# The order of the last steps before the output projection: scores of attention heads 2 and 3 ahead of the projection of the values

## The chip, the cores and the metric

The kernel runs on one core of one Trainium2 chip. The metric is the device time of one execution in microseconds (us), compared by the median of several runs. The engines are PE (TensorE: matmuls, PEld for its weight loads), DVE (VectorE), ACT (ScalarE), POOL (GpSimd) and SP (SyncE, which here issues nearly all DMAs).

## The reference

One layer of a sequence encoder on 512 tokens of 2048 features. The input is scaled and shifted by vectors computed from a condition `c` (a matrix product with `ada_w`), projected by `w_in`, and the projection is cut into the inputs of four mixers of 512 features each. Their outputs are concatenated, projected by `w_out`, gated, added to the input and normalised; a feed-forward block follows.

```python
h = x * (1.0 + scale1) + shift1
proj = h @ w_in[l]
...
o_a = _hgrn2(...)            # cat[0:4]   four heads of 128
o_b = _s5(...)               # cat[4:8]
o_c = _stick_breaking(sb_q, sb_k, sb_v)   # cat[8:12]  four heads of 128
o_d = _rwkv7(...)            # cat[12:16]
mix = jnp.concatenate([o_a, o_b, o_c, o_d], axis=-1) @ w_out[l]
x = _layer_norm(DEEPNORM_ALPHA * x + gate1 * mix, ln1_g[l], ln1_b[l])
```

The mixer that the change touches is the third, in blocks of 128 queries:

```python
z = einsum('bhtd,bhsd->bhts', q, k)          # q already times 128 ** -0.5
log_rest = where(mask, log_sigmoid(-z), 0)   # mask: key before query
after = cumsum(log_rest, reverse=True) - log_rest
w = where(mask, exp(log_sigmoid(z) + after), 0)
o = einsum('bhts,bhsd->bhtd', w, v)
```

## The kernel before, in words

All matrices are float32. A projection is made of three matmuls for each pair of tiles: both operands are split into a rounded part and a rest (`hi` by an ACT cast, `lo` by a DVE subtraction), and `mm3` (L592) multiplies hi by hi, lo by hi and hi by lo. `wload` (L580) loads a 256 KB piece of weights by one DMA from SP into one of three buffers `wr`, then splits it into `wh` and `wl`, three buffers each.

The kernel is written as a list of steps, the string `ORDER` (L40, L41), and the loop at L1456 issues them in that order; a number behind a colon is `E.rate`. The program's instructions are then ordered by a planner: an instruction has the place at which it was issued as its priority, `high_priority(offset=n)` moves it n places ahead, and on each engine the planner takes, by its own estimate of times, the first in priority of those that are ready and have a buffer. An engine then works through its own list strictly in that order. Weight loads and splits stand 500 places ahead (`E.ahead`), the four heads of the first mixer 1500 (`BEFORE`, "H").

The steps around the change:

- `K<h>`: `qk(h)` (L1396), queries and keys of attention head h. Two calls of `proj_fm` (L1172), each 48 matmuls into one PSUM bank `pd` with 4 weight loads; the banks are emptied by ACT into `qT` and `kT` in the pool `pp` (16 buffers).
- `VS`: `proj_tm` (L1184) for the values of all four heads: 192 matmuls with 16 weight loads, four `pd` banks (all there are) held from the first to the last, emptied by four ACT copies into `tm` (pool `pp`). In the trace its matmuls read `pd<-wh,hh` and the like, those of `K<h>` `pd<-hh,wh`.
- `A<p>`: `sb_scores` (L1007) for heads 2p and 2p+1. Matmuls of 16 records in five banks `pm` give the scores, which ACT copies into five tiles `sz`; DVE adds the mask, ACT takes Abs, Exp and Ln into five tiles `sl`, DVE makes max and sum, sums them up by scans and subtracts, ACT takes the last Exp. The two small tiles `one` make all Ln wait for the last Exp before them, and the last Exp for the scans. The tiles `sz` and `sl` are ten of the 34 buffers of the pool `tp`; `sz` is kept for `B<p>`.
- `B<p>`: `sb_values` (L1049): 20 transposes of `sz`, copied by ACT to `swT`, and matmuls of 40 records with the values; the result is `cat[8+2p]` and the next.
- `H<h>`: a head of the first mixer. Seven levels, each a DVE subtraction `hd`, two ACT Exp into `hx`, two DVE products, 4 matmuls (in eight records) and a masked DVE copy into `hP`. `L<p>` takes their logarithms (ACT Ln) ahead of that. `TAIL` (`hg_tail`, L993) normalises the four outputs.
- The condition's product with `ada_w` is a queue `E.bg` of 224 entries: 192 steps of one DMA `aw` and one DVE operation `acc` each, 12 ends, and 20 empty ones. `pump` (L1154) hands out `E.rate` entries behind every weight load of a projection; `PUMP` empties the queue. An end takes a `pd` bank for a moment.
- `W1`, `W2`: `w_out` (L1420). For each of four column blocks, four `pd` banks take eight (W1) or four (W2) tiles of `cat`; DVE multiplies each bank by the gate into `go` and adds it to `acc`, which frees the bank.

By the rates in `ORDER`, 168 of the 224 entries are handed out up to and including `K0`.

Of the kernel before, what the change touches and what calls it, by code (L numbers as in the profile page):

```python
# [37 lines left out]
START = "M0 E0 G0 C0 g2 M1 S0 g6 F0 M2 S1 g1 E1"  # L38

ORDER = ("k3 xg:3 r1:1 v1 k2:1 v3 r3:3 v0:2 S5 r2 r0:1 KEYS SUB INV v2:3 V:1 R12:3 R4:3 CHAIN F2:1 F1:2 F3:1 "  # L40
         "R0:2 F0 K1:2 L0 H0 H1 K0:2 L1 H2 H3 VS:2 A0 K3:2 K2:2 PUMP TAIL B0 A1 W1:2 B1 W2")  # L41

BEFORE = {"S5": 600, "KEYS": 600, "SUB": 300, "INV": 1000, "CHAIN": 1500, "H": 1500}

# [1811 lines left out]
```

## Time and profile before

| | us |
|---|---|
| median of 3 runs | 2546.42 (2540.97 to 2553.87) |
| profiled execution, its own time | 2543.48 |
| its span, first to last instruction | 2541.5 |
| PE busy | 2437.8 |
| DVE busy | 1730.7 |
| ACT busy | 955.5 |
| mean granted TensorE clock | 0.980 |

Matmuls overlap, so busy PE time is more than the time the matrix unit needs for them; a matmul of 512 columns lasts 0.39 us and the next starts 0.23 us after it. "Idle before, releaser" behind a row is time in which the engine did nothing before it, and what ended that.

In the span, `K1` and `K0` end with the copies of their keys at 724.6 and 766.5 us, the four heads `H0` to `H3` run from about 712 to 833 us, `VS` from 755 to 833 us, `A0` begins at 835 us, `K3` and `K2` run from 833 to 885 us, the score matmuls of `A1` stand at 896 to 901 us, and `W1` has its first matmul at 890.9 us.

### The profile page before, as it was taken

To read this page: it belongs to the slowest core of one execution; us is meant where nothing else is said; L and a number is where in the kernel's file an instruction comes from. 1 tells how busy PE (TensorE), PEld (TensorE's weight loads), DVE (VectorE), ACT (ScalarE), POOL (GpSimd) and SP (SyncE) were. 2 spreads that over 40 slices of the span, in tenths; PEclk is the share of its full clock that TensorE was granted. 3 is DMA by queue.
4 is the path that set the end of the run, shared out by engine and by line. 5 is a ranking of instruction groups with operands and counts; after the bars stand their busy time and mean duration, and the time that the engine had idled before them with its cause. 6 is when DMAs were issued, how large, how long until landed. Compare 5 with 4: busy or idle time off the path is not lost. (4 is left out here: it accounts for less than half of the span.)

```text
span 2541.5 us, 33306 instructions
## 1 busy us (share of the span) xinstructions
PE 2437.8 (96%) x11890; PEld 1897.7 (75%) x11890; DVE 1730.7 (68%) x2673; ACT 955.5 (38%) x1406; POOL 131.4 (5%) x293
## 2 busy tenths in 40 slices
PE   8999999999999999989999999999999999999996
PEld 3557767776788778867777877787778788788885
DVE  3755987357689975788787778777877744536227
ACT  2435242322454654164444444434443421121122
POOL 3300000010000000000000000000000000000000
PEclk9999999899999999999999999999999999999998
DMA  9876324334744554336666566655665788869632
GB/s 294 258 245 199 92 75 126 103 116 145 227 130 137 167 173 133 125 100 208 219 208 206 180 203 214 201 182 197 208 204 192 258 321 294 300 206 315 225 117 82
DMA packets 328877, 481.83 MB, mean 190 GB/s; under 512 B 44962, under 2 KB 151676, under 8 KB 328712
## 3 DMA queue, kind: packets, MB, share of 16 engines
q1 hardware_dynamic: 317976, 452.78, 55.3%
q0 software_dynamic: 8480, 26.27, 2.7%
q8 instruction: 93, 1.52, 0.3%
q10 hardware_dynamic: 2256, 0.67, 0.1%
q14 instruction: 72, 0.59, 0.1%
HBM read 445.51 MB, written 34.10 MB: 189 GB/s over the span
## 5 line engine op out<-in xcount | busy, mean ns | idle before, releaser
L102 ACT CAST wh<-wx 128x1024 fp32r<-128x1024 f32 (+1 forms) x416 | 401.2, 970 | 735.9 <-PE p L93 348.7
L105 DVE TENSOR_TENSOR wl<-wx,wh 128x1024 fp32r<-128x1024 f32 (+1 forms) x416 | 457.5, 1119 | 264.4 <-ACT wh L102 262.1
L102 ACT CAST wh<-wr 128x512 fp32r<-128x512 f32 x236 | 145.5, 618 | 329.2 <-PE pd L93 224.7
L123 DVE SCALAR_TENSOR_TENSOR acc<-aw,cact,acc 128x512 f32<-128x512 f32 x240 | 179.8, 749 | 123.6 <-DMA aw<-in_ada_w_dram 120.3
L93 PE MATMUL pt<-wl,gh 128*128 128x512 f32 x640 | 249.3, 390 | 2.1 <-DVE wl L105 1.8
L93 PE MATMUL pt<-wh,gh 128*128 128x512 f32 x640 | 249.1, 389 | 0.0
L93 PE MATMUL pt<-wh,gl 128*128 128x512 f32 x640 | 249.0, 389 | 0.0
L105 DVE TENSOR_TENSOR wx<-wx 128x512 f32<-128x512 f32 (+1 forms) x264 | 225.1, 866 | 28.6 <-DMA wx<-in_ffn_w_dram 26.9
L105 DVE TENSOR_TENSOR wl<-wr,wh 128x512 fp32r<-128x512 f32 x236 | 162.0, 689 | 113.3 <-ACT wh L102 96.2
L93 PE MATMUL pd<-hh,wl 128*128 128x512 f32 x512 | 205.6, 402 | 5.6 <-DVE wl L105 5.5
L93 PE MATMUL pd<-hh,wh 128*128 128x512 f32 x512 | 207.6, 407 | 2.4 <-ACT hh L102 2.4
L93 PE MATMUL pd<-hl,wh 128*128 128x512 f32 x512 | 204.0, 399 | 0.0
L93 PE MATMUL p<-wl,hdh 128*128 128x512 f32 x352 | 140.6, 404 | 20.0 <-DVE wl L105 20.0
L93 PE MATMUL p<-wh,hch 128*128 128x512 f32 x336 | 137.1, 408 | 16.4 <-DVE g L105 12.3
L93 PE MATMUL p<-wh,hdh 128*128 128x512 f32 x352 | 141.8, 403 | 1.1 <-ACT u L102 1.1
L93 PEld LDWEIGHTS pt<-wl,gh 128*128 128x128 f32 x640 | 120.1, 188 | 28.6 <-DVE wl L105 4.0
L93 PE MATMUL p<-wh,hdl 128*128 128x512 f32 x352 | 141.3, 402 | 0.0
L93 PEld LDWEIGHTS pt<-wh,gh 128*128 128x128 f32 x640 | 120.2, 188 | 25.6 <-ACT wh L102 0.8
L93 PEld LDWEIGHTS pt<-wh,gl 128*128 128x128 f32 x640 | 120.2, 188 | 25.1
L93 PE MATMUL p<-wl,hch 128*128 128x512 f32 x336 | 135.7, 404 | 0.3 <-DVE wl L105 0.3
L93 PE MATMUL p<-wh,hcl 128*128 128x512 f32 x336 | 135.0, 402 | 0.0
L93 PE MATMUL p<-wl,hbh 128*128 128x512 f32 x336 | 132.2, 393 | 0.8 <-DVE wl L105 0.8
(530 smaller groups left out, 4535.3 us busy)
## 6 DMA issues: line engine op xcount, KB each, us to landing
wx<-in_ffn_w_dram SPq DMA_DIRECT2D x592, 256.0 KB, 3.4
aw<-in_ada_w_dram SPq DMA_DIRECT2D x384, 256.0 KB, 4.6
wr<-in_w_in_dram SPq DMA_DIRECT2D x184, 256.0 KB, 3.3
wx<-in_ffn_w_dram SPq DMA_DIRECT2D x44, 1024.0 KB, 6.1
gh<-gd SPq DMA_DIRECT2D x88, 256.0 KB, 5.3
gl<-gd SPq DMA_DIRECT2D x88, 256.0 KB, 6.2
wr<-in_w_out_dram SPq DMA_DIRECT2D x64, 256.0 KB, 3.0
gd<-gh POOLq DMA_DIRECT2D x44, 256.0 KB, 4.1
```

Source lines behind the costliest of these rows:

```text
L93: return self.nc.tensor.matmul(out=out, lhsT=lhsT, rhs=rhs, start=start, stop=stop, **kw)
L102: self.nc.scalar.copy(out=out, in_=in_)
L105: self.nc.vector.tensor_tensor(out=out, in0=a, in1=b, op=op)
L123: self.nc.vector.scalar_tensor_tensor(out=out, in0=a, scalar=s, in1=b, op0=op0, op1=op1)
```

## The change

`VS` is taken from behind `H3` and put behind `TAIL`; `A1` is taken from behind `B0` and put behind `K2`. Nothing else is changed: every step, its rate and its code stay.

```diff
 ORDER = ("k3 xg:3 r1:1 v1 k2:1 v3 r3:3 v0:2 S5 r2 r0:1 KEYS SUB INV v2:3 V:1 R12:3 R4:3 CHAIN F2:1 F1:2 F3:1 "
-         "R0:2 F0 K1:2 L0 H0 H1 K0:2 L1 H2 H3 VS:2 A0 K3:2 K2:2 PUMP TAIL B0 A1 W1:2 B1 W2")
+         "R0:2 F0 K1:2 L0 H0 H1 K0:2 L1 H2 H3 A0 K3:2 K2:2 A1 PUMP TAIL VS:2 B0 W1:2 B1 W2")
```

So the steps behind `H3` read: before `VS A0 K3 K2 PUMP TAIL B0 A1 W1`, after `A0 K3 K2 A1 PUMP TAIL VS B0 W1`.

## Prediction

> **What bounds the kernel now.** I read the page first, for the engine whose list fills the span.
>
> ```profile
> span 2541.5 us, 33306 instructions
> PE 2437.8 (96%) x11890; PEld 1897.7 (75%) x11890; DVE 1730.7 (68%) x2673; ACT 955.5 (38%) x1406; POOL 131.4 (5%) x293
> ```
>
> PE is the bound, so the change is worth the idle PE time that it takes away or adds, no more. The second view is therefore who made PE wait; of its rows these lie near the moved steps.
>
> ```profile
> PE pd L93 <- ACT sz L99: 5.1, 1, 5.1
> PE pm L96 <- DVE ho L105: 2.0, 2, 1.3
> ```
>
> The columns are total, times and longest. The first is one wait, the longest single one in that view, and it stands beside `A1`. The timeline of PE there, and that of DVE in the same microseconds:
>
> ```profile
> 921.98 0.39 PE L93 MATMUL pd<-wl,cath 128*128 128x512 f32 x1
> 927.51 0.76 PE L93 MATMUL pd<-wh,cath 128*128 128x512 f32 x1 [5.14 <-ACT sz L99]
> 928.08 0.63 PE L93 MATMUL pd<-wh,catl 128*128 128x512 f32 x1
> ...
> 931.92 0.50 PE L93 MATMUL pd<-wh,catl 128*128 128x512 f32 x1
> 932.26 0.39 PE L93 MATMUL pd<-wl,cath 128*128 128x512 f32 x1
> 932.48 0.39 PE L93 MATMUL pd<-wh,cath 128*128 128x512 f32 x1
> ```
>
> ```profile
> 919.55 2.96 DVE L126 TENSOR_TENSOR_SCAN sl<-ones,sl 128x256 f32<-128x256 f32 x4
> 922.43 0.13 DVE L118 TENSOR_SCALAR one<-sl 128x1 f32<-128x1 f32 x1
> 922.47 0.69 DVE L105 TENSOR_TENSOR sz<-sz,sl 128x512 f32<-128x512 f32 x1
> ...
> 923.67 2.50 DVE L105 TENSOR_TENSOR sz<-sz,sl 128x512 f32<-128x512 f32 x4
> 926.08 0.69 DVE L105 TENSOR_TENSOR wl<-wr,wh 128x512 fp32r<-128x512 f32 x1
> 926.68 1.29 DVE L105 TENSOR_TENSOR go<-pd,g 128x512 f32<-128x512 f32 x2
> ```
>
> The releaser named on PE's row is the exponential of `A1`, but no matmul of `W1` reads it. What PE needs at 927.51 is an empty bank: the first column block of `W1` has filled all four `pd`, and the operation that empties them, `go`, stands on DVE behind the scans and subtractions of `A1`, which come earlier in `ORDER` and so have the better priority. `go` starts at 926.68, its first half ends near 927.4, and PE goes on. After the pause matmuls follow each other by 0.43 us until 931.92 (928.08, 928.50 and so on), and by 0.23 us from 932.26.
>
> The other wait, a little earlier:
>
> ```profile
> 885.17 1.14 PE L93 MATMUL pm<-rs,selC 32*128 32x512 f32 x8
> 887.63 1.25 PE L96 MATMUL pm<-ident,sz 128*128 128x128 f32 x8 [1.32 <-DVE ho L105]
> 889.61 1.53 PE L96 MATMUL pm<-ident,sz 128*128 128x128 f32 x12 [0.73 <-DVE ho L105]
> ```
>
> `TAIL` fills the `pm` banks with its broadcasts (`rs,selC`), DVE empties them by the products `ho`, and the transposes of `B0` wait for them. The projections are over at 885, so PE has little else.
>
> **The change part by part.**
>
> *`A1` ahead of `W1` by the length of `VS`.* `A1` needs `K2`, and before it had only `B0` and the first block of `W1` beside it.
>
> ```profile
> 896.49 4.48 PE L93 MATMUL pm<-kT,qT 128*128 128x512 f32 x16
> ```
>
> From these score matmuls to the resumed matmul at 927.51 the chain takes 31 us. Afterwards `K2` should end near 838 (`K3` and `K2` take the place of `VS`, which ended at 833, and `A0`'s scores add 4.5), and `A1` near 869. `VS` follows it with 192 matmuls, 44 us at 0.23, then `B0` and the first block of `W1`, and only then the first `go`, with DVE free of `A1`. Gained: the idle 5.14 us, and the slow restart: 11 starts from 927.51 to 932.26 took 4.75 us, where 0.23 us apiece make 2.50, so 2.25 us.
>
> *`VS` behind `TAIL`.* The broadcasts of `TAIL` and the products `ho` now have `VS` on PE beside them, so the transposes of `B0` find their banks free: gained 1.32 + 0.73 = 2.05 us. If `TAIL` came too late for that cover, these 2.05 would stay.
>
> *What fills PE under the heads.* Until 833 `VS` was the filler between the levels of `H1` to `H3`; now `K3` and `K2` are.
>
> ```profile
> core 0: us, PE busy (x) PEld busy (x) DVE busy (x) ACT busy (x) POOL busy (x), PEclk, DMA share, GB/s
> 767.00:835.00 68.00, 68.00 (x386) 56.51 (x384) 60.40 (x116) 31.64 (x68) 0.53 (x1) 1.00 0.46 134
> 835.00:890.00 55.00, 52.69 (x241) 41.12 (x241) 50.46 (x93) 35.77 (x61) 0.00 (x0) 1.00 0.58 176
> 890.00:928.00 38.00, 32.75 (x164) 26.28 (x163) 33.65 (x62) 29.58 (x50) 0.00 (x0) 0.96 0.59 190
> ```
>
> Both fillers have 192 matmuls, 16 DMAs of 256 KB on SP, 16 casts on ACT and 16 subtractions on DVE, at the same spacing: nothing on PE, and on SP's queue 16 loads exchanged for 16. The queue of `ada_w`: 168 entries are gone before, and the next 32 (with 32 DMAs `aw` on SP and 32 `acc` on DVE) go beside `K3` and `K2` instead of `VS`, again under the heads; `PUMP` finds 24 entries, of which two are steps and two ends, so hardly anything comes out in one heap. POOL's queue has no part in it. Cost: zero, hidden by the same fillers; if that cover failed, a late load would cost PE what it is late.
>
> *`A0` under `H2` and `H3`.* This is the new load. Its inputs are there at 766.5:
>
> ```profile
> L102 ACT COPY kT<-pd x1: 581/581/581, 766.5 to 766.5; 128x512 f32<-128x512 f32 x1
> 835.00:871.00 36.00, 12.60 (x20) 9.05 (x15) 1.00 0.62 190
> L105 DVE TENSOR_TENSOR sz<-sz,negm x16: 284/288/294, 837.1 to 905.2; 128x128 f32<-128x128 f32 x16
> L102 ACT COPY sz<-pm x10: 586/586/592, 836.5 to 901.0; 128x512 f32<-128x512 f32 x10
> L99 ACT ACTIVATE sz<-sz,one x10: 707/718/725, 867.0 to 926.8; 128x512 f32<-128x512 f32 x10
> ```
>
> The second row is the stretch in which `A0` ran, for the instructions on the tiles `sl` alone (DVE 12.60, ACT 9.05); the other rows are for `A0` and `A1` together, in ns, so half of each is added: 8 x 0.288 = 2.3 for DVE and 5 x 0.586 + 5 x 0.718 = 6.5 for ACT. That is 15 us of DVE and 16 of ACT. From 767 to 835 DVE has 68 - 60.40 = 7.6 us free, ACT 36. So the heads and `A0` together end some 8 us later than the heads did alone. PE does not pay for that as such: what it lacks in head matmuls it takes from the 384 filler matmuls of `K3`, `K2`, `VS`. The heads' result is needed by `W2` only, behind the 384 matmuls of `W1` (88 us at 0.23).
>
> But ACT's functions get mixed. What a change of function costs:
>
> ```profile
> 846.24 0.63 ACT L99 ACTIVATE sl<-sl 128x512 f32<-128x512 f32 x1
> 846.89 1.28 ACT L99 ACT_TABLE_LOAD   x1
> 848.19 0.72 ACT L99 ACTIVATE sl<-sl,one 128x512 f32<-128x512 f32 x1
> ...
> 862.84 1.28 ACT L99 ACT_TABLE_LOAD   x1
> ```
>
> A load ahead of the first Ln, another ahead of the next Exp. Before 846.89 the last load is at 706.88: no Ln stood among the Exps of the heads. There, where two loads stood just ahead of a head (`H0`), PE waited for its first level:
>
> ```profile
> 703.61 1.28 ACT L99 ACT_TABLE_LOAD   x1
> 706.88 1.28 ACT L99 ACT_TABLE_LOAD   x1
> 714.14 1.10 PE L93 MATMUL pm<-hx 128*128 128x64 f32 x8 [1.98 <-DVE hx L105]
> ```
>
> PE's list is fixed, eight filler matmuls (1.9 us) between two levels, so it can't go on with a filler when a level is late. Bounds: no cost, if the five Ln of `A0` fall behind the last head or between two heads; at most five pairs of loads, 10 x 1.28 = 12.8 us, if each Ln has a head's Exp on both sides and PE pays every load. Below nothing there is no room, since PE was busy all 68 us of that window. I take one pair at the nearest row's price, 1.98 us, since the five Ln become ready together and ACT is less than half busy. The Trainium skill, "ScalarE: Activation LUTs", section "What ACT_TABLE_LOAD costs", gives 2.66 us for a switch with its drain; by that the upper bound would be 26.6 us, an estimate from that page. The rows above do not agree: the operation before the load was over by then (846.24 + 0.63), and the next starts 1.30 us behind the load's start. The same page, "Table sets: the hidden batching unit", knows a set with both exp and ln, by which the cost would be zero; the two loads around the Ln of `A0` show that this program does not use it.
>
> *Handovers.* `VS` now hands its four `pd` banks to `W1`. Its ACT copies `tm` are of the form of `sz<-pm` (0.586), and the last matmuls of the four banks are 0.7 us apart; the 20 transposes of `B0` (1.25 + 1.53 us in the rows above) lie between. Cost zero, if ACT is free of `A1` then. The buffers of `tp`: `A1`'s five `sl` are free 40 us before the 16 `acc` of `W1` want them, before they were not.
>
> **The sum**, against the profiled execution's own 2543.48: -5.14 - 2.25 - 2.05 + 1.98 = -7.46, which makes 2536.0. The median of the runs lies 2.94 above that execution, so the forecast of the median is 2539.0.
>
> **The rivals.**
>
> *The wait moves.* If `A0` and the heads crowd each other so much that `A1` starts 15 us late, it ends near the end of `VS`, and ACT's copies `tm` or DVE's first `go` stand behind it as they do now. Then only the 2.05 us go: 2544.4. For it: DVE lacks 8 us in the window. Against: 8 is half of 15, and `K2` needs only PE and the splits, which stand 500 places ahead.
>
> *The heads' Exps are cut by Ln: slower.* Place: levels of `H2` and `H3` from 768 on. Price 1.28 us a load on PE; with ten, -9.44 + 12.8 = +3.4, 2549.8. It decides against the change from eight loads on (9.44 / 1.28 = 7.4). For it: ACT is idle 36 us of 68 between the pairs of `hx`, so Ln fits there one by one, and PE's list has no slack. Against: the planner may place Ln in one group. By the skill's price of a switch, named above, this rival would end at 2563.6, an estimate.
>
> *Nothing is moved in effect.* The planner works by readiness, so if `A0` finds no ten buffers in `tp` beside the heads, its chain starts at 835 as before, `A1` follows later, and the gain is the 2.05 of `TAIL` or less: 2544.4 to 2546.4. For it: a head has some ten tiles in `tp`, the finished outputs and gates another dozen. Against: `A1` would still have `VS` behind it.
>
> **How the numbers follow.** Forecast 0.5, the wait moves 0.15, Ln among Exp 0.2, nothing in effect 0.15. 0.5% is 12.7 us, about what a measurement of this kernel can tell from no change; -7.46 and all rivals lie within it. Faster than that needs the full 9.44 and another 3 us, which the spread of the runs (5.45 below the median) or a further wait that falls away could give: 0.16. Slower by that needs the far end of the Ln rival and more: 0.08. Range: low by the full gain and that spread, 2546.42 - 9.44 - 5.45 = 2531.5; high by the Ln rival, 2549.8, and a little beyond, 2551.
>
> **What would show it.** Right: no PE wait over 1 us between 835 and 950; `go` of `W1` directly behind the last matmul of its bank; score matmuls of `A1` followed by `pd<-wh,hh`; `TAIL`'s products beside `VS`. Wrong: more than four table loads between 767 and 880 with PE waits for `hx` in `H2` and `H3`; a wait for `tm` or `go` at the first matmuls of `W1`; `A0` still at 835. The far parts (feed-forward) should keep their length; if they don't, the planner has changed more than these steps, and the sum says nothing of that.

## The result and the profile after

| | median, us | profiled execution | its span |
|---|---|---|---|
| before, 4 runs | 2546.26 (2540.97 to 2553.87) | 2543.48 | 2541.5 |
| after, 4 runs | 2581.81 (2574.28 to 2586.52) | 2582.68 | 2580.7 |

The ratio is 1.0137, with a 95% interval of 1.0115 to 1.0158. The change made the kernel slower by 35.6 us; the forecast was a gain of 7.5. The page of the kernel after, its span and PE's row:

```profile
span 2580.7 us, 33297 instructions
PE 2444.7 (95%) x11890; PEld 1901.5 (74%) x11890; DVE 1733.1 (67%) x2673; ACT 956.0 (37%) x1406; POOL 131.4 (5%) x293
```

PE has the same 11890 instructions and DVE the same 2673, so the 39.2 us of span are not more work. Who made PE wait (total, times, longest) now begins with a row that the kernel before does not have:

```profile
PE pd L93 <- DVE acc L123: 30.8, 1, 30.8
```

That is one wait of 30.8 us. PE's timeline around it:

```profile
832.80 1.04 PE L93 MATMUL pm<-hsq,ones 128*32 128x512 f32 x2
833.78 2.42 PE L93 MATMUL pm<-kT,qT 128*128 128x512 f32 x7
...
844.13 0.95 PE L93 MATMUL pd<-ones,acc 128*128 128x1 f32 x8
846.28 3.72 PE L93 MATMUL pm<-kT,qT 128*128 128x512 f32 x12 [1.20 <-ACT kT L102]
851.23 1.13 PE L93 MATMUL pm<-kT,qT 128*128 128x256 f32 x4 [1.24 <-ACT sz L102]
883.16 1.87 PE L93 MATMUL pd<-ones,acc 128*128 128x1 f32 x8 [30.79 <-DVE acc L123]
884.89 0.77 PE L93 MATMUL pd<-wh,hh 128*128 128x512 f32 x1
```

`hsq,ones` at 832.80 is the end of `H3`, and `A0`'s scores follow it; they did not go under the heads. `K2` is over at 844, `A1`'s scores at 852. Then PE does nothing until `pd<-ones,acc`, an end of the `ada_w` queue, and right behind the end stand the first matmuls of `VS` (`pd<-wh,hh`). `VS` is the only large work left for PE there, and its first weights were long ready: the first three splits `wl` of `VS` ended at 840.3, 843.9 and 847.0 (with three buffers there can be no more). What it lacked, by this reading, was a bank: `VS` holds all four `pd`, and the end, which the `PUMP` ahead of it had issued, was to have one of them first. The experiments below test that. DVE shows why the end came so late:

```profile
851.97 5.83 DVE L126 TENSOR_TENSOR_SCAN sl<-ones,sl 128x512 f32<-128x512 f32 x8
...
869.89 0.75 DVE L123 SCALAR_TENSOR_TENSOR acc<-aw,cact,acc 128x512 f32<-128x512 f32 x1
870.55 3.09 DVE L123 SCALAR_TENSOR_TENSOR sl<-sz,sl 128x512 f32<-128x512 f32 x5
873.56 5.83 DVE L126 TENSOR_TENSOR_SCAN sl<-ones,sl 128x512 f32<-128x512 f32 x8
879.31 0.13 DVE L118 TENSOR_SCALAR one<-sl 128x1 f32<-128x1 f32 x1
879.35 3.09 DVE L105 TENSOR_TENSOR sz<-sz,sl 128x512 f32<-128x512 f32 x5
882.36 0.74 DVE L123 SCALAR_TENSOR_TENSOR acc<-aw,cact,acc 128x512 f32<-128x512 f32 x1
```

The scans at 851.97 are `A0`'s, those at 873.56 `A1`'s. Between the chains go the steps `acc` of the queue, and the last of them, which completes the end's sum, comes behind `A1`'s whole chain, which stands ahead of `PUMP` in the order: at 882.36. So PE waited for a condition vector's sum behind 11.8 us of score arithmetic. By stretches (the column before the DMA share is the granted clock):

```profile
853.00:883.00 30.00, 0.00 (x0) 0.00 (x0) 29.25 (x55) 18.77 (x29) 0.00 (x0) 0.55 0.22 70
883.00:890.00 7.00, 6.84 (x20) 5.78 (x21) 5.12 (x11) 0.28 (x2) 0.00 (x0) 0.50 0.11 37
890.00:935.00 45.00, 45.00 (x212) 36.66 (x212) 21.00 (x33) 19.88 (x36) 0.00 (x0) 1.00 0.34 101
```

In the first row PE is busy for 0.00 us and DVE for 29.25 of 30: for these 30 us DVE sets the time. In the second PE works at a clock of 0.50. Further on, the waits that the prediction meant to remove are indeed gone; the same places in `B0` and `W1` now read:

```profile
932.33 2.35 PE L96 MATMUL pm<-ident,sz 128*128 128x128 f32 x20
...
961.84 0.47 PE L93 MATMUL pd<-wh,cath 128*128 128x512 f32 x1 [0.52 <-ACT wh L102]
964.75 0.51 PE L93 MATMUL pd<-wh,cath 128*128 128x512 f32 x1 [0.36 <-DVE go L105]
```

The 20 transposes have no wait (1.32 + 0.73 before), and the wait for `go` is 0.36 (5.14 before).

To compare stretches, call "the stage" the time from the first head matmul `pm<-hx` to the first `pd<-woh`, which belongs to the last part of `w_out`: the attention heads' four tiles of `cat`, behind `W2`. Before it is 714.14 to 1046.09, 332.0 us; after, 715.88 to 1078.88, 363.0. From the last matmul of the heads (834.28 and 832.80) to `pd<-woh` it is 211.8 and 246.1, 34.3 more, and that adds up: the wait 30.79; the restart at half clock 3.5 (the end took 1.73 to its successor where another took 0.81, and 12 matmuls from 884.89 to 890.15 took 5.26 where 0.227 apiece make 2.72); two waits at the scores of `A1` 1.20 + 1.24; 30 filler matmuls more left behind the heads, 6.8 (26 of `K2` and 192 of `VS` against 188); less 5.14 - 0.36, 2.25 and 2.05 gained. The sum is 34.4. What lies outside the stage is 2209.5 us of the span before and 2217.7 after, and between 2203 and 2224 in the other profiled executions below (one apart, which changes code there), so single spans say less than the stage does.

### The profile page after: what moved, and what is told of

It reads as the page before. It is cut to its first block, busy times and chain, and to the rows that moved or that the text cites. A ratio compares the mean times of both kernels' runs of the same rounds, so it can differ in the third digit from the quotient of the medians.

```text
span 2580.7 us, 33297 instructions
## 1 busy us (share of the span) xinstructions
PE 2444.7 (95%) x11890; PEld 1901.5 (74%) x11890; DVE 1733.1 (67%) x2673; ACT 956.0 (37%) x1406; POOL 131.4 (5%) x293
## 4 chain that ended last, share of the span: by engine, by line
PE 48%; issue 32%; DVE 8%; DMA 7%; POOL 2%; SPq 1%; ACT 1%; DVEq 0%; POOLq 0%; ACTq 0%
PE pd L93 19%; PE pt L93 12%; PE pm L93 12%; DMA aw<-in_ada_w_dram 6%; PE p L93 4%; DVE wl L105 2%; POOL gd L1632 1%; DVE acc L123 1%; DMA wx<-in_ffn_w_dram 1%; SPq L1719 1%; DVE acc L105 1%; PE pm L96 1%; DVE sl L126 0%; POOL hgmf L231 0%; POOL hgmf L233 0%
## 5 line engine op out<-in xcount | busy, mean ns | idle before, releaser
L93 PE MATMUL p<-wh,hch 128*128 128x512 f32 x336 | 136.9, 407 | 18.2 <-DVE g L105 11.2
L93 PEld LDWEIGHTS pt<-wl,gh 128*128 128x128 f32 x640 | 120.1, 188 | 27.2 <-DVE wl L105 2.2
L93 PEld LDWEIGHTS pt<-wh,gl 128*128 128x128 f32 x640 | 120.1, 188 | 25.0
```

What stands on the lines that cost most here:

```text
L93: return self.nc.tensor.matmul(out=out, lhsT=lhsT, rhs=rhs, start=start, stop=stop, **kw)
```

## The experiments

Theory 1 was formed on the trace after: a pool gives its buffers in the order of the steps, not to whoever is ready, so `VS` waited for the end's bank, and the end for DVE behind the chains. The rivals named in the expectations are other places for the loss. Ratios are to the kernel before on the same chip; the medians come from several chips. Lists of PE's waits are for the stretch from 826 to 1050 us, behind the heads.

**The queue's end behind VS.** Only the order is changed, against the kernel after:

```diff
-A0 K3:2 K2:2 A1 PUMP TAIL VS:2 B0
+A0 K3:2 K2:2 A1 TAIL VS:2 PUMP B0
```

> The changed kernel with PUMP moved behind VS, so that the last ends of the ada_w queue stand behind the values in the list and no longer between A1 and VS. Theory 1 (banks in order): a pool grants its buffers in the order of the steps; VS could not take a pd bank before the last end had taken one, and that end waits for a sum that DVE makes behind the chain of A1. Then the wait of 30.8 us is gone, VS follows K2 at once, and the time is 2537 to 2547. Theory 2 (DVE is full): the chains of A0 and A1, one directly behind the other, hold up the splits of VS's weights, whatever the ends do; then 15 us or more of waits for wl stay, 2560 or more.

2552.90 us, ratio 1.0020 (1.0006 to 1.0033). The stage takes 332.9. PE's three longest waits:

```profile
PE pd L93 <- DVE wl L105: 1.6, 1, 1.6
PE pm L93 <- DVE mod L123: 1.6, 1, 1.6
PE pm L93 <- ACT sz L102: 1.2, 1, 1.2
```

The 30.8 are gone, as the first theory has it, but the median lies 6 us above the upper end that it gave. The stage is level with before, and the profiled execution has its surplus outside (2220.0 against 2209.5); why is left open.

**Only the end's bank.** The order after is kept whole, and the result of an end goes to a bank of `pm`:

```diff
         acc = st["acc"]
-        ps = E.psd()
+        ps = E.psm()
```

> The changed kernel with its order as it is; only the bank that an end of the ada_w queue takes comes from the pool pm instead of pd. Theory 1 (banks in order): VS needs no pd bank behind an end any more and runs beside the chains of A0 and A1, though the last end is still just as late on DVE; 2537 to 2548, no PE wait over 5 us between 833 and 950. Theory 2 (DVE is full): the chains delay the splits, 2560 or more. Theory 3 (PE takes its list in order of steps and an end is simply ahead of VS in it, whichever bank it uses): the wait of some 30 us stays, about 2580.

2544.95 us, ratio 0.9998 (0.9981 to 1.0015); the stage 333.0. This is the cleanest run: no step is moved, PE, DVE and ACT have as many instructions as in the kernel after, and the median is 36.9 us lower. `VS` starts at 837.2, between the score matmuls of `A0` and of `A1`. So the loss came through the bank: an end that stood ahead of `VS` in PE's list whatever its bank, the third theory, would have kept the wait. And yet the gains forecast (9.4) are not there. PE's waits now:

```profile
PE pm L93 <- DVE one L120: 2.4, 1, 2.4
PE pm L93 <- DVE rs L105: 1.6, 1, 1.6
PE pm L96 <- DVE ho L105: 1.2, 1, 1.2
PE pm L93 <- ACT sz L102: 0.6, 1, 0.6
PE pd L93 <- DVE go L105: 0.4, 1, 0.4
```

They sum to 6.2, against 7.9 in the same stretch before (`sz` 5.1, `ho` 2.0, `go` 0.5, `wl` 0.3). The last end still stops PE behind DVE, `TAIL`'s rsqrt (`rs`) comes late because `A1`'s chain is now ahead of it, and the restart costs again:

```profile
870.47 1.05 PE L93 MATMUL pm<-ones,acc 128*128 128x1 f32 x8 [2.39 <-DVE one L120]
868.00:871.00 3.00, 0.61 (x6) 0.53 (x5) 2.58 (x8) 2.74 (x4) 0.00 (x0) 1.00 0.62 228
871.00:875.00 4.00, 4.00 (x14) 3.29 (x14) 2.95 (x5) 3.11 (x6) 0.00 (x0) 0.57 0.61 208
```

**The same bank in the order before**, as a control:

> The kernel before, with only the bank of the end of the ada_w queue changed from pd to pm. Theory (the bank costs only where a step that is ready stands behind an end in the order; in the kernel before VS stands ahead of the ends): no change, 2541 to 2551, the stage 330 to 334. Rival (an end on pd costs in itself in any order): 2535 or less, or, if pm is the scarcer pool here, 2555 or more.

2547.06 us, ratio 1.0008 (0.9986 to 1.0031), the stage 711.6 to 1045.01, 333.4, the old waits still there (`sz` 4.0, `ho` 2.1). The bank is worth nothing where `VS` stands ahead of the ends, so it is the meeting of the two, as theory 1 has it.

**One half of the change at a time.** Only `VS` moved, `A1` behind `B0` as before:

```diff
-A0 K3:2 K2:2 A1 PUMP TAIL VS:2 B0 W1:2
+A0 K3:2 K2:2 PUMP TAIL VS:2 B0 A1 W1:2
```

> The other half: VS behind TAIL, A1 where it was before (behind B0). Theory 1 (banks in order): VS still waits for the last end's bank, but the end's sum does not stand behind A1 any more; PE waits from the end of K2 (845) to the end of the queue of loads and sums (about 870), 20 to 25 us; the wait of go in W1 behind A1 is back. 2563 to 2574. Theory 2 (two chains on DVE are needed for the loss): about as before, 2540 to 2550.

2580.40 us, ratio 1.0131 (1.0104 to 1.0159). Too high for the expectation, which had credited `A1` with a larger part of the wait.

```profile
PE pd L93 <- DVE acc L123: 27.2, 1, 27.2
PE pd L93 <- ACT sz L99: 4.1, 1, 4.1
```

With `A1` out of the way the end comes at 873.92 instead of 883.16, but PE also stops earlier, without `A1`'s scores. Moving `VS` alone thus makes a loss as large as the whole change, and the old wait behind `A1` is back at 4.1.

Only `A1` moved, `VS` behind `H3` as before:

```diff
-H2 H3 A0 K3:2 K2:2 A1 PUMP TAIL VS:2 B0
+H2 H3 VS:2 A0 K3:2 K2:2 A1 PUMP TAIL B0
```

> Half of the change: A1 directly behind K2, VS where it was before (behind H3). Theory 1: nothing is left for PE between A1 and W1 but B0, so the chain of A1 runs beside the first block of W1 as before, go waits behind it: the wait near 5 us and a time of 2541 to 2550, like before. Theory 2 (A1 directly behind A0 on DVE is what costs): 2560 or more.

2559.75 us, ratio 1.0050 (1.0032 to 1.0068), the stage 351.1. The first theory, a time like before, does not hold; the measured time lies at the edge of the second theory's range. It is a loss of its own, by two waits:

```profile
919.98 2.09 PE L93 MATMUL pm<-rs,selC 32*128 32x512 f32 x8 [11.21 <-DVE rs L105]
...
945.36 0.79 PE L93 MATMUL pd<-wh,cath 128*128 128x512 f32 x1 [7.98 <-DVE go L105]
944.61 1.29 DVE L105 TENSOR_TENSOR go<-pd,g 128x512 f32<-128x512 f32 x2 [5.75 <-DMA g<-gate]
```

The first wait is `A1`'s doing: on DVE its chain stands ahead of `TAIL`'s rsqrt and ends at 912.5, the rsqrt then lasts until 919.8, and PE, with no projection left to cover it, waits 11.2 us for both. The second is not the old wait for `go`, though it bears the same name: DVE itself is idle ahead of `go` and waits 5.75 us for the load of the gate. That load is issued at 937.61, where the kernel before issues its first at 913.90. Its tile comes from the pool `tp`, as those of `TAIL` and `B0` do; whether that is why it is late was not tested.

**The queue ahead of A1.** The kernel after with `PUMP A1 TAIL VS:2` instead of `A1 PUMP TAIL VS:2`:

> The changed kernel with PUMP ahead of A1 instead of behind it: the last sums of the ada_w queue go ahead of A1's chain on DVE, the ends still stand ahead of VS. Theory 1 (the last sum stands behind A1 on DVE): the end comes about 12 us earlier, near 870; the wait is 14 to 21 us and the time 2563 to 2573. Theory 2 (A0's chain and the loads aw set the end): the wait stays at 26 to 31 us, 2577 to 2584.

2575.75 us (two executions), ratio 1.0105 (1.0078 to 1.0132), between the two expectations. The stage is 353.1, 9.9 less than after, and the wait is shorter by about `A1`'s chain:

```profile
872.58 1.66 PE L93 MATMUL pd<-ones,acc 128*128 128x1 f32 x7 [20.11 <-DVE acc L123]
```

30.79 - 20.11 = 10.7 beside 11.8 us of chain (870.55 to 882.36 above). So of the 30.8 about a third was `A1`; the other 20 lie beside `A0`'s chain and the queue's remaining steps, which DVE does in turn.

**The queue emptied earlier.** The kernel after with higher rates for the projections long before, so that no entry is left at `PUMP`:

```diff
-CHAIN F2:1 F1:2 F3:1
+CHAIN F2:3 F1:3 F3:3
```

> The changed kernel with higher rates at F2, F1 and F3 (3 each instead of 1, 2 and 1), so that the ada_w queue is empty before A0 and no end stands between A1 and VS; banks and order of the steps are as in the change. Theory 1 (the late end before VS is the whole loss): the wait of 30.8 us is gone, 2538 to 2552. Theory 2 (the loss goes elsewhere): the sums now stand beside the projections of F1 to F3, where PE waits for wl already, and cost there what they save here, 2555 or more.

2586.20 us, ratio 1.0147 (1.0119 to 1.0174), as the second theory has it. The wait in front of `VS` is gone indeed, but the loss is elsewhere. The heads start at 731.63, 15.8 us later than after. Part of that is the steps `acc`, which now hold up the projections `F`: from 600 us to the heads PE waits 11.3 us, 5.3 of them for `acc` and 2.9 for `he`, where the kernel after has 5.9 us of waits. The DMA share from 640 to 715 us is 0.83, where the kernel before has 0.75; the rest of the 15.8 was not traced. And the last end of the queue now falls into the heads:

```profile
795.47 1.97 PE L93 MATMUL pm<-hx 128*128 128x64 f32 x8 [6.98 <-DVE hx L105]
...
806.82 1.81 PE L93 MATMUL pd<-ones,acc 128*128 128x1 f32 x8
808.49 0.77 PE L93 MATMUL pd<-hh,wh 128*128 128x512 f32 x1
```

From 787 to 807 there is not one filler matmul between the levels of the head, and the first one (`pd<-hh,wh`, a key or query) comes directly behind the end. That is what the same rule would do at another place, with another step as the victim; it was not tested there by itself.

**Where A0 can go.** Two runs on the step "`A0` under `H2` and `H3`". First, the kernel after with `A0`'s scores in banks `pd` (`E.psd()` instead of `E.psm()` in `sb_scores`):

> The changed kernel with the score matmuls of A0 and A1 written to banks of pd instead of pm, so that A0's first matmuls need not stand behind the heads' banks. It asks why A0 did not run under the heads. Theory 1 (every pool grants its buffers in the order of the steps, tp too): four score banks are filled near 768, but ACT can't copy them, because the tiles sz stand behind all tiles of H2 and H3 in tp; the four pd banks are held until the heads are over, K3 and K2 get none, and PE has no filler under H2 and H3: idle for 25 us or more between 765 and 835, 2590 to 2630. Theory 2 (only the pm banks held A0 back): the copies sz follow at once, the chain of A0 is over when the heads are, and the wait before VS shrinks to about 15 us: 2560 to 2570.

One execution, 2593.38 us, in the first theory's range. The scores now begin under the heads, and there too the queue of a pool is kept:

```profile
770.72 1.12 PE L93 MATMUL pd<-kT,qT 128*128 128x512 f32 x2 [0.75 <-ACT kT L102]
...
780.30 1.97 PE L93 MATMUL pm<-hx 128*128 128x64 f32 x8 [4.47 <-DVE hx L105]
...
841.13 1.13 PE L93 MATMUL pd<-kT,qT 128*128 128x256 f32 x4
```

ACT's first copy `sz` of these scores comes at 839.99, 68 us behind the first of their matmuls; the likely reason is that the tiles `sz` stand behind those of `H2` and `H3` in `tp`. So the four banks stay full, `A0`'s last scores wait until `H3` is over (841.13), and `K3`, behind them in the order, gets no bank until then (its first matmul is at 842.48): PE waits 23.9 us for `hx` in 14 places, where before it waited once, 1.98.

Second, the kernel before with `A0` put ahead of `H2` in the order, and nothing else:

> The kernel before, with the first pair's scores (A0) moved ahead of the heads H2 and H3 and nothing else, so that they are taken where the prediction saw them. Theory 1 (as the prediction had it: they lie beside the heads' work at the price of one table pair): A0's scores near 767, the last head matmul at most 3 us later than in the kernel before (834.28 with its start at 714.14), 2541 to 2549. Theory 2 (the rival of the cut heads: DVE is at 106.8 of 120 us there, so A0's chain of some 12 us pushes the heads): the last head matmul 8 to 16 us later and part of it lost on PE, 2550 to 2562.

2551.64 us, ratio 1.0012 (0.9995 to 1.0029). The median lies in the second theory's range, but the ratio can't be told from no change, so the time decides nothing; the trace says more.

```profile
769.05 4.58 PE L93 MATMUL pm<-kT,qT 128*128 128x512 f32 x16
782.59 1.28 ACT L99 ACT_TABLE_LOAD   x1
787.60 1.28 ACT L99 ACT_TABLE_LOAD   x1
790.25 1.08 PE L93 MATMUL pm<-hx 128*128 128x64 f32 x8 [2.75 <-DVE hx L105]
837.54 4.93 DVE L126 TENSOR_TENSOR_SCAN sl<-ones,sl 128x512 f32<-128x512 f32 x6
```

Now the scores are where the prediction saw them. It is the place in the order that brought `A0` there, not its readiness. Its five Ln go in one group with one pair of table loads, as the prediction took it, and PE's wait behind the second load is 2.75 us beside its 1.98. But the chain is not under the heads even so: seven of its eight scans come between 837.5 and 843.4, at the heads' end, and its last Exps from 844.3.

The last head matmul is at 841.66 with the first at 711.77, so the heads take 129.9 us instead of 120.1, 9.8 more. That this is near the 8 us that the prediction worked out from DVE's free time is luck, since DVE is busy for 111.9 of the 129.9 and has not run out of time. PE's own list accounts for most of it: 4.6 us of score matmuls that ran behind the heads before, the wait of 2.75, and 1.7 us by the slow clock after it (0.67 from 790.25 to 794 and 0.88 to 798). The stage is 343.8. Further on PE waits 4.4 us for an end of the queue (`acc`, 883.30), with projection matmuls directly behind it; that was not followed up.

**A1 behind W1.** The kernel before with `A1` later still, `B0 W1:2 A1 B1`:

> The kernel before with A1 moved the other way, behind W1; VS and PUMP as before. It asks by itself for the first term of the prediction: that go of W1's first block stands behind A1's chain on DVE. Theory 1: the wait of 5.14 us and the slow restart of 2.25 us are gone, the rest as before, and A1 runs beside W2: 2537 to 2543. Theory 2 (the chain of A1 is late for B1 then): PE waits for B1 or at the end of W2, 2550 or more.

2560.44 us, ratio 1.0044 (1.0027 to 1.0061).

```profile
1017.67 2.61 PE L96 MATMUL pm<-ident,sz 128*128 128x128 f32 x11 [10.17 <-ACT sz L99]
```

`B1`'s transposes now wait 10.2 us for `A1`'s last Exp: what `W1` no longer pays (5.14), `B1` pays twice, and a wait of 2.6 for `go` is left. The second theory's range held.

**The best of what was learnt.** The order after with `PUMP TAIL A1 VS:2`, and the ends on `pm`:

> The order after, with the second pair's scores put behind TAIL (K2, PUMP, TAIL, A1, VS) and the result of an end of the ada_w queue taken from a bank of pm instead of pd. Theory (banks are granted in the order of the steps, and the end held VS's bank): no wait before VS, TAIL's rsqrt and products are no longer behind A1's chain on DVE, so the waits rs 1.59 and ho 1.17 of the run with the bank alone go to under 0.5, the sz wait stays under 1; the stage from the first head matmul to the first woh matmul is 325 to 330 us where the kernel before has 332.0; 2535 to 2543. Rival (what A1 does not meet at TAIL it meets at B0): waits for ho, sz or go of 3 us or more in B0 and W1, the stage 332 to 342, 2544 to 2556.

2548.66 us, ratio 1.0010 (0.9992 to 1.0028). The rival's time and stage held (339.4), but not the waits that it named: none in `B0` or `W1` is over 2 us, and the longest is once more for the queue's last end:

```profile
PE pm L93 <- DVE acc L123: 4.3, 1, 4.3
PE pd L93 <- DVE go L105: 1.8, 1, 1.8
PE pd L93 <- ACT tm L102: 1.8, 2, 1.5
```

The theory is right that the wait for `rs` goes away; the clock of 0.50 from 882 to 888 us, behind the 4.3, is the restart.

No version tried beats the kernel before by more than the noise.

## Why the prediction was wrong

- *What fills PE under the heads.* This step failed. It priced the rest of the queue at zero, because `PUMP` finds few entries ("hardly anything comes out in one heap"). The number of entries was not the point: the two ends take a bank each, from the four that `VS` holds as long as it runs, and `VS` had been moved behind them. That was worth 30.8 us of idle PE and 3.5 us of restart. Changing the bank alone brought the ratio from 1.0137 to 0.9998. Nor did the queue's steps run "again under the heads": 20 of its operations `acc` came behind 833 us, where the heads were over, the last of them at 882.36 behind the chains of `A0` and `A1`, and the last end needed it.
- *The planner works by readiness.* This is the assumption below that step, written out in the rival "Nothing is moved in effect". It holds for engines: an instruction that is ready may pass one that isn't, as `VS` passes the last end once that has a bank in `pm`. For buffers it does not: steps that were ready, whole stretches of filler among them, waited for a bank of `pd` that was promised to an earlier, unready step. The prediction asked what stands behind what on engines and in DMA queues; of the pools it looked at `tp` and at who gets the banks of `VS`, and never at whom `VS` has to wait for in `pd`.
- *`A0` under `H2` and `H3`.* This failed too, for the same reason as far as the runs show: `A0` came at 833.78, as at 835 before; with banks of `pd`, or with a place ahead of `H2`, its scores came at 770. "`A0` still at 835" was on the list of what would show it wrong. With `A0` and `A1` both behind the heads, 24 us of DVE chains (12.5 and 11.8) came almost in one piece; the prediction had put the first of them under the heads. So `A1` ended at 883 and not near 869. The table loads, and so the rival of the cut Exps, never came into it: from 767 to 883 there are four, all behind the heads.
- *`A1` ahead of `W1` by the length of `VS`* and *`VS` behind `TAIL`* were right in their mechanism: 5.14 became 0.36, and the transposes of `B0` have no wait. In the run with the end on `pm`, where nothing else hides them, the stage still gained nothing (333.0 beside 332.0): the end's 2.4, `rs` 1.6, `ho` 1.2 and `sz` 0.6 with a slow restart took the place of most of the 9.4. `A1`'s chain left `W1` and came to stand ahead of `TAIL`'s rsqrt, which the sum had at nothing. The rival "The wait moves" was the right picture for that, though not with the waits it named.
- *The chances.* Slower by over 0.5% had 0.08, from one rival on ACT. No rival looked at a resource that the moved step holds from its first to its last matmul; the paragraph on handovers asked to whom `VS` gives its four banks, and not from whom it gets them.

## What to carry to other kernels

Before a step is moved in a list, ask of each pool it draws on who stands ahead of it there at the new place, and when that one will be ready; a step that takes all of a small pool waits for the slowest of those ahead. A small product in the wrong pool can stop the largest filler, and giving it a buffer elsewhere is a one-word change. And where a wait of 5 us stands behind a 12 us chain on another engine, moving the chain moves the wait: none of the places tried for `A1` made the kernel faster.

## What the runs showed of the hardware

The length of a pause alone did not decide whether PE's granted clock fell. In the kernel before a pause of 1.98 us (to 714.14) left it at 1.00. In the kernel after one of 2.27 us (to 715.88) was followed by 0.50 from 717 to 719; in the run with the end on `pm` one of 2.39 us, with the clock at 1.00 up to 871, was followed by 0.57 over the next four microseconds; and in the run with `PUMP` behind `VS` one of 1.56 us (to 896.39) was followed by 0.50 from 898 to 902. In the kernel after the clock is 0.55 over the 30 us of idle time: if it knows only 1.00 and 0.50, that is a drop about 3 us after 853, or 3.6 after the last matmul's end. The Trainium skill, "TensorE: Matmul & The Clock Gate", section "What's actually happening", has half rate after an idle window of about 3.4 us that runs freely; the long pause agrees with that, the short ones do not as it is put. It also has full rate after about 3.4 us of sustained work; here PE stayed slow for 4.75 us in the kernel before (927.51 to 932.26) and for 7.0 in the kernel after (883.16 to 890.15).
